# A hybrid attention, SSM and MoE block: masks behind the first rows, own tiles for the second half of x, two tiles for C, three for uT

## The chip, the cores and the metric

The kernel runs on one core of a Trainium2 chip. The metric is the device time of one execution in microseconds; the median of three executions of the kernel before is 1205.27 us (1204.71, 1205.27 and 1208.66). TensorE (PE) runs at one of two clock levels, 1.2 or 2.4 GHz; a view by stretches of time gives the clock that was granted, as a share of the higher one.

## The reference

One block over x of 1024 rows (S) by 1024 columns (D), all in float32:

```python
h = _rmsnorm(x, norm_mix_g[l])
z = h @ w_in[l]
q, k, v, f, u_ssm, g_attn, g_ssm = jnp.split(z, splits, axis=-1)
...
y_attn = _forgetting_attention(q, k, v, f + b_forget[l]).reshape(b, s, D_ATTN)
y_ssm = _s5(u_ssm, ...)
mixed = (jax.nn.sigmoid(g_attn) * (y_attn @ w_proj_attn[l])
         + jax.nn.sigmoid(g_ssm) * (y_ssm @ w_proj_ssm[l]))
x = x + mixed @ w_out[l]
x = x + _hier_moe(_rmsnorm(x, norm_ffn_g[l]), ...)
```

The forgetting attention has 8 heads of 64; its logits take the running sum over time of log sigmoid of f. The S5 part has 32 groups of 16 channels with 64 complex states each, driven by u and read out by the complex matrix C. The MoE has 32 experts of width 256, two for each row.

## The kernel before, in words

A product in full precision is made of three matmuls: each operand is split into a high part (rounded to fp32r) and a low part, and high by high, low by high and high by low are added up in PSUM. So x after its norm is kept transposed as `hTh[k]` and `hTl[k]` (k = 0 to 7, 128 columns of D each), and every weight as a pair such as `wuh` and `wul`.

The front (lines 104 to 260) loads x in eight row tiles of 128 x 1024 (`x_load`, four buffers). `normalize` does for each tile: sum of squares on ACT (line 203), the mean on DVE (204), the power on POOL (206, `rstd`), the multiplication on DVE (207). `turn_x` transposes the four row tiles of one half at one k on PE (line 212, through PSUM tiles `psB_t`), ACT writes `hTh` (213), DVE writes `hTl` (214). `split_u` splits the weights of u (lines 221 to 224). `products_u` makes u^T for one k and one half of the rows: four m by three matmuls (229 to 231, tiles `psA_t`) and two for the forget logits (232, 233). ACT and DVE are put in the written order within the first half (`manual_schedule`); everywhere else a scheduler orders each engine's instructions by its own priorities.

The second half of x uses the same four buffers, so its loads stand behind the first half's transposes. From line 263 on come the coefficients of the SSM on DVE and ACT (`exp_acc`, `wrap`, sines at 342), the two parts of C (lines 351 to 361: `cin`, one buffer, transposed on PE at 359), then the products of the second half, and `store_u`, which copies u from PSUM to `uS` (DVE 242, ACT 244) and the forget logits to `FL` and `Fa` (245, 246). Four stores write `uS` to `u_d` (451). The forget sums (459 to 483) work on 8 partitions: exponential, logarithm, a scan over time.

The SSM stage (486 to 613) has four blocks b of 8 groups. `load_u(b)` brings u back as `uT` in eight DMAs (498); `uT` has two buffers, so block b + 2 is loaded at the end of block b. DVE, POOL and ACT build for each block phases `v`, `w`, sines `SI` and cosines `CO` (516 to 524), and the matrices `HQ` and `PT` (535 to 537, with `tq` on POOL); PE transposes `PT` (575), ACT copies it to `Pm` (579), PE multiplies `uT` by it (582), DVE turns the result (562, 564), scans it (594) and turns it back (`zc`), and PE reads it out (602, 603). Sixteen runs of the gate products (`gate_run`, lines 182 to 184, 48 matmuls each, results `ge` copied by ACT at 186) stand between these on PE, with `wgh` and `wgl` split from `raw_g` (171, 172). Behind follow the GLU, the attention, the output projection and the MoE. SP issues most DMAs, in order.

Of the kernel before, what the change touches and what calls it, by code (L numbers as in the profile page):

```python
# [10 lines left out]
F32 = mybir.dt.float32  # L11
# [31 lines left out]
def hybrid_block(ctx: ExitStack, tc: tile.TileContext, t, out):  # L43
# [63 lines left out]
    def x_load(i):  # L107
        x_ = xp.tile([P, D], F32, name="x", bufs=4)
        nc.sync.dma_start(x_, t["x"][i * P:(i + 1) * P, :])
        return x_  # L110
# [9 lines left out]


# [3 lines left out]
    for o in range(2):  # L125
# [10 lines left out]

    tri = cp.tile([P, P], F32, name="tri")
    nc.gpsimd.memset(tri, 1.0)
    nc.gpsimd.affine_select(tri, tri, pattern=[[1, P]], compare_op=ALU.is_gt, fill=0.0,
                            base=0, channel_multiplier=-1)  # L140

    mask_s = cp.tile([P, 256], BF16, name="mask_s")
    nc.gpsimd.memset(mask_s, 0.0)
    nc.gpsimd.affine_select(mask_s, mask_s, pattern=[[1, 256]], compare_op=ALU.is_ge, fill=NEG,
                            base=-128, channel_multiplier=-1)

    mask_m = cp.tile([P, P], BF16, name="mask_m")
    nc.gpsimd.memset(mask_m, 0.0)
    nc.gpsimd.affine_select(mask_m, mask_m, pattern=[[-1, P]], compare_op=ALU.is_ge, fill=NEG,
                            base=0, channel_multiplier=1)  # L150
    bfor = cp.tile([H, 1], F32, name="bfor")
    nc.gpsimd.dma_start(bfor, t["b_forget"].rearrange("(p o) -> p o", o=1))

    gk2 = cp.tile([P, 1], F32, name="gk2")
    gqt = cp.tile([P, 1], F32, name="gqt")
    for o in (0, 64):
        nc.gpsimd.dma_start(gk2[o:o + 64], t["k_norm_g"].rearrange("(p o) -> p o", o=1))
        nc.gpsimd.dma_start(gqt[o:o + 64], t["q_norm_g"].rearrange("(p o) -> p o", o=1))
# [31 lines left out]
    uS = [xp.tile([P, 8, P], F32, name=f"uS{m}") for m in range(4)]  # L190
# [3 lines left out]
    nc.gpsimd.memset(f32(wf), 0.0)  # L194
    FL = fp.tile([H, S], F32, name="FL")
    Fa = fp.tile([H, S], F32, name="Fa")
# [51 lines left out]
    with tc.manual_schedule(engines={mybir.EngineType.Activation, mybir.EngineType.DVE}):  # L248
        normalize(xs)
        for k in range(KD):  # L250
            if k % 2 == 0:
                split_u(k)
            first_half = turn_x(xs, k, halves[0])
    xs = [x_load(i) for i in range(4, NT)]
# [97 lines left out]
    for nm, dst in (("ssm_C_re", Cre), ("ssm_C_im", Cim)):  # L352
        cin = tp.tile([P, 4, 2, 64], F32, name="cin")
        src = t[nm].rearrange("(b a) c p -> (a c) b p", a=8)
        nc.sync.dma_start(cin[:, :, 0, :], src)
        nc.sync.dma_start(cin[:, :, 1, :], src)
        ps = smtile()
        for b in range(4):
            nc.tensor.transpose(ps[:, b * P:(b + 1) * P],
                                cin[:, b].rearrange("q o p -> q (o p)"), ident)  # L360
        nc.scalar.copy(dst.rearrange("p g c -> p (g c)"), ps)
# [64 lines left out]
    for k in range(5, KD):  # L426
        products_u(k, pu, pf, halves[0])
        turn_x(xs, k, halves[1])
    store_u(pu, pf, 0)
# [56 lines left out]
    with ExitStack() as st:  # L486
# [8 lines left out]
        def load_u(b):  # L495
            uT = wp2.tile([P, GB, P], F32, name="uT", bufs=2)
            for tau in range(8):
                nc.sync.dma_start(uT[CG * tau:CG * tau + CG],
                                  u_d[b * P:(b + 1) * P, tau, :].rearrange("(g c) j -> c g j", c=CG))
            uTs.append(uT)  # L500

        load_u(0)
        load_u(1)
        for m in range(3):
            gate_run(m)
        for b in range(G // GB):
# [102 lines left out]
            if b < 2:  # L609
                load_u(b + 2)  # L610
# [905 lines left out]
```

## Time and profile before

| what | value |
|---|---|
| median of three executions | 1205.27 us |
| the profiled execution's own time | 1208.14 us |
| its span in the profile | 1206.4 us |
| PE busy | 1116.5 us (93%) |
| DVE busy | 793.5 us (66%) |
| ACT busy | 619.5 us (51%) |
| POOL busy | 432.1 us (36%) |
| read from and written to HBM | 164.30 and 35.52 MB |

The profile is one execution. Busy time of PE counts matmuls whose ends are modelled and overlap; a share of 93% over the span is a mean over stages. The waits of an engine are listed by what released it, and the timeline gives each instruction's start with the idle time before it in brackets.

### The profile page before, as it was taken

The page shows a single profiled execution, that of the slowest core. Times are in us where ns is not written, and L with a number is a line of the kernel's source. Part 1 is how long each engine was busy: PE and PEld are TensorE (multiplying, and loading weights), DVE is VectorE, ACT ScalarE, POOL GpSimd, SP SyncE. Part 2 cuts the span into 40 slices and gives each one's busy share as a digit, 9 for nine tenths or more (in the row PEclk, how much of TensorE's full clock was granted, in tenths as well). Part 3 has the DMA queues.
Part 4 walks back from the last instruction along what each step waited for, and adds up shares of the span by engine and source line. Part 5 has one row for each costly group of instructions (what it writes and reads, how often), then busy time and mean ns, then how long its engine had stood idle before and what let it go on. Part 6 is the DMA issues. An engine that isn't in the chain of part 4 may idle for free. (4 is left out here: it accounts for less than half of the span.)

```text
span 1206.4 us, 15940 instructions
## 1 busy us (share of the span) xinstructions
PE 1116.5 (93%) x5323; PEld 854.3 (71%) x5324; DVE 793.5 (66%) x1561; ACT 619.5 (51%) x1195; POOL 432.1 (36%) x431
## 2 busy tenths in 40 slices
PE   5899899899999999999899988998499999999995
PEld 4678778687898778888677777886366666666562
DVE  4657577667025889898987696538566666666661
ACT  5423332332335576766769553103366666666662
POOL 3025445432514474656714362103322222222211
PEclk9899899999999999999989999999699999999998
DMA  8516435330253012000622539564599999999992
GB/s 234 82 41 157 92 75 104 80 91 28 87 121 53 2 27 47 11 23 28 210 70 101 175 124 346 189 220 179 185 306 341 333 312 317 312 310 320 310 332 51
DMA packets 100919, 193.78 MB, mean 161 GB/s; under 512 B 26177, under 2 KB 55169, under 8 KB 100833
## 3 DMA queue, kind: packets, MB, share of 16 engines
q1 hardware_dynamic: 82176, 150.16, 40.8%
q0 software_dynamic: 14048, 34.17, 10.5%
q10 hardware_dynamic: 4608, 8.39, 1.9%
q8 instruction: 43, 0.70, 0.2%
q14 instruction: 44, 0.35, 0.1%
HBM read 164.30 MB, written 35.52 MB: 166 GB/s over the span
## 5 line engine op out<-in xcount | busy, mean ns | idle before, releaser
L1102 DVE TENSOR_TENSOR wel<-raw_e,weh 128x512 fp32r<-128x512 f32 x256 | 157.4, 684 | 118.8 <-ACT weh L1101 107.5
L1101 ACT CAST weh<-raw_e 128x512 fp32r<-128x512 f32 x256 | 137.0, 621 | 3.0 <-DMA raw_e<-in_w_expert_up 1.8
L910 POOL TENSOR_TENSOR sm<-sm,pe 128x256 f32<-128x256 f32 (+2 forms) x80 | 96.4, 1205 | 72.5 <-ACT pe L907 64.2
L1377 PE MATMUL psA_t<-wd,hT 128*96 128x512 f32 x256 | 117.4, 600 | 3.1 <-DMA wd<-in_w_expert_down 2.3
L1352 PE MATMUL psA_t<-weh,xh 128*96 128x512 f32 x256 | 103.7, 405 | 0.2
L1353 PE MATMUL psA_t<-wel,xh 128*96 128x512 f32 x256 | 102.0, 399 | 0.0
L183 PE MATMUL psA_t<-hTh,wgl 128*128 128x512 f32 x256 | 101.9, 398 | 0.0
L182 PE MATMUL psA_t<-hTh,wgh 128*128 128x512 f32 x256 | 101.4, 396 | 0.0
L1354 PE MATMUL psA_t<-weh,xl 128*96 128x512 f32 x256 | 101.2, 395 | 0.0
L184 PE MATMUL psA_t<-hTl,wgh 128*128 128x512 f32 x256 | 100.8, 394 | 0.0
L1379 POOL DMA_INDIRECT out_rows<-R,ix x32 | 46.1, 1441 | 128.5 <-ACT hT L1368 117.2
L793 PE MATMUL psA_t<-wqh,hTh 128*128 128x384 f32 x256 | 88.3, 345 | 0.0
L794 PE MATMUL psA_t<-wql,hTh 128*128 128x384 f32 x256 | 86.8, 339 | 0.0
L795 PE MATMUL psA_t<-wqh,hTl 128*128 128x384 f32 x256 | 86.8, 339 | 0.0
L1328 POOL DMA_INDIRECT XG<-xn_d,ix x32 | 36.5, 1140 | 139.7 <-PE psB_t L1339 132.3
L1378 ACT ACTIVATE R<-psA_t,wts 96x512 f32<-96x512 f32 x64 | 43.7, 682 | 77.1 <-PE psA_t L1377 75.0
L1377 PEld LDWEIGHTS psA_t<-wd,hT 128*96 128x96 f32 x256 | 40.4, 168 | 56.4 <-issue 49.0
L905 ACT ACTIVATE pH<-psB_t 128x512 fp32r<-128x512 f32 (+1 forms) x96 | 49.1, 512 | 38.9 <-PE psB_t L902 38.7
L908 DVE TENSOR_TENSOR pL<-pe,pH 128x256 fp32r<-128x256 f32 (+2 forms) x80 | 62.9, 798 | 6.8 <-ACT pe L907 5.9
L855 DVE TENSOR_REDUCE mx<-psB_t 128x1 f32<-128x512 f32 (+2 forms) x96 | 51.2, 550 | 7.9 <-PE psB_t L850 4.2
L183 PEld LDWEIGHTS psA_t<-hTh,wgl 128*128 128x128 f32 x256 | 48.7, 190 | 9.5 <-POOL wgl L172 0.2
L184 PEld LDWEIGHTS psA_t<-hTl,wgh 128*128 128x128 f32 x256 | 48.5, 189 | 9.5
(427 smaller groups left out, 2878.2 us busy)
## 6 DMA issues: line engine op xcount, KB each, us to landing
raw_e<-in_w_expert_gate SPq DMA_DIRECT2D x64, 512.0 KB
raw_e<-in_w_expert_up SPq DMA_DIRECT2D x64, 512.0 KB
wd<-in_w_expert_down SPq DMA_DIRECT2D x64, 512.0 KB
gate_d<-ge ACTq DMA_DIRECT2D x32, 256.0 KB
gt<-gate_d SPq DMA_DIRECT2D x16, 512.0 KB
raw_g<-in_w_in SPq DMA_DIRECT2D x12, 512.0 KB
raw_q<-in_w_in SPq DMA_DIRECT2D x48, 128.0 KB
x<-in_x SPq DMA_DIRECT2D x8, 512.0 KB
```

What stands on the lines that cost most here:

```text
L182: nc.tensor.matmul(ps, wh, hTh[k][:, ns], start=(k == 0), stop=False)
L183: nc.tensor.matmul(ps, wl, hTh[k][:, ns], start=False, stop=False)
L184: nc.tensor.matmul(ps, wh, hTl[k][:, ns], start=False, stop=(k == KD - 1))
L793: nc.tensor.matmul(ps[:, :384], ah, wh, start=(k == 0), stop=False)
L794: nc.tensor.matmul(ps[:, :384], ah, wl, start=False, stop=False)
L910: nc.gpsimd.tensor_tensor(sm[:, o0:], sm[:, o0:], pe[:, :n], ALU.add)
L1101: nc.scalar.copy(wh[d_], src)
L1102: nc.vector.tensor_tensor(wl[d_], src, f32(wh[d_]), ALU.subtract)
L1352: nc.tensor.matmul(ps, xh[:, k, :], wh[:, k % 2, :], start=(k == 0), stop=False)
L1353: nc.tensor.matmul(ps, xh[:, k, :], wl[:, k % 2, :], start=False, stop=False)
L1354: last = nc.tensor.matmul(ps, xl[:, k, :], wh[:, k % 2, :], start=False, stop=(k == KD - 1))
L1377: pe = nc.tensor.matmul(po, hT[:, j, :], wd[j][:, ns], start=(j == 0), stop=(j == 1))
```

## The change

It does five things. (1) The four row tiles of the second half of x get their own buffers, in a ring (`tag="uS"`) that the four `uS` tiles take over once the last transposes have read them; their loads are issued straight behind those of `raw_u`. (2) The POOL work for `tri`, `mask_s`, `mask_m` and the five small POOL DMAs (`bfor`, `gk2`, `gqt`) is written behind the first half, and the zeroing of `wf` behind the first half's `normalize`. (3) `FL` and `Fa` become rows 0 to 7 and 32 to 39 of one tile. (4) `cin` gets two buffers. (5) `uT` gets three buffers: blocks 0 to 2 are loaded ahead of block 0, block 3 at the end of block 0.

```diff
     def x_load(i):
-        x_ = xp.tile([P, D], F32, name="x", bufs=4)
+        x_ = xp.tile([P, D], F32, name="x" if i < 4 else "x2", tag="x" if i < 4 else "uS", bufs=4)
         nc.sync.dma_start(x_, t["x"][i * P:(i + 1) * P, :])
...
+    xs2 = [x_load(i) for i in range(4, NT)]
...
-    tri = cp.tile([P, P], F32, name="tri")
...
-    uS = [xp.tile([P, 8, P], F32, name=f"uS{m}") for m in range(4)]
+    uS = []
...
-    nc.gpsimd.memset(f32(wf), 0.0)
-    FL = fp.tile([H, S], F32, name="FL")
-    Fa = fp.tile([H, S], F32, name="Fa")
+    FL = fp.tile([64, S], F32, name="FL")
+    FL, Fa = FL[0:H], FL[32:32 + H]
...
         normalize(xs)
+        nc.gpsimd.memset(f32(wf), 0.0)
...
-    xs = [x_load(i) for i in range(4, NT)]
+
+    tri = cp.tile([P, P], F32, name="tri")
...
+    xs = xs2
...
-        cin = tp.tile([P, 4, 2, 64], F32, name="cin")
+        cin = tp.tile([P, 4, 2, 64], F32, name="cin", bufs=2)
...
+    uS.extend(xp.tile([P, 8, P], F32, name="uS", tag="uS", bufs=4) for m in range(4))
     store_u(pu, pf, 0)
...
-            uT = wp2.tile([P, GB, P], F32, name="uT", bufs=2)
+            uT = wp2.tile([P, GB, P], F32, name="uT", bufs=3)
...
-        load_u(0)
-        load_u(1)
+        for b in range(3):
+            load_u(b)
...
-            if b < 2:
-                load_u(b + 2)
+            if b < 1:
+                load_u(b + 3)
```

The scheduler then orders the first stages anew. ACT in the first half, before (`hTh_151` to `hTh_154` are k = 4 to 7; `x` with line 203 is the second half):

```order
L213 ACTIVATE hTh_151<-psB_t,gmix 128x512
L213 ACTIVATE hTh_152<-psB_t,gmix 128x512
L221 CAST wuh<-raw_u 128x1024
L222 CAST wf<-raw_u 128x2x8
L213 ACTIVATE hTh_153<-psB_t,gmix 128x512
L203 ACTIVATE junk,ss<-x 128x1024
L213 ACTIVATE hTh_154<-psB_t,gmix 128x512
L203 ACTIVATE junk,ss<-x 128x1024 x3
```

In these rows the second half's squares follow k = 6 and 7. The same place of ACT after the change (`hTh_136` to `hTh_139` are k = 2 to 5; `x_109` to `x_115` are the second half's tiles):

```order
L190 ACTIVATE hTh_136<-psB_t,gmix 128x512
L180 ACTIVATE junk,ss<-x_109 128x1024
L190 ACTIVATE hTh_137<-psB_t,gmix 128x512
L180 ACTIVATE junk,ss<-x_111 128x1024
L198 CAST wuh<-raw_u 128x1024
L199 CAST wf<-raw_u 128x2x8
L190 ACTIVATE hTh_138<-psB_t,gmix 128x512
L180 ACTIVATE junk,ss<-x_113 128x1024
L190 ACTIVATE hTh_139<-psB_t,gmix 128x512
L180 ACTIVATE junk,ss<-x_115 128x1024
```

The squares of the second half now stand between k = 2 and 5 of the first, each ahead of a later `hTh`. PE at the transposes of the second part of C, before (`hTh_152` is k = 5, `hTh_153` k = 6):

```order
L232 MATMUL psB_t<-hTh_152,wf 128x512
L233 MATMUL psB_t<-hTl_160,wf 128x512
L229 MATMUL psA_t<-hTh_153,wuh 128x512
L230 MATMUL psA_t<-hTh_153,wul 128x512
L359 MATMUL psB_t<-ident,cin 128x128 x4
L212 MATMUL psB_t<-ident,x 128x128 x4
L231 MATMUL psA_t<-hTl_161,wuh 128x512
```

Four transposes of `cin` stand inside k = 6. PE at both parts of C after the change (`hTh_138` is k = 4, `hTh_139` k = 5):

```order
L209 MATMUL psB_t<-hTh_138,wf 128x512
L210 MATMUL psB_t<-hTl_146,wf 128x512
L189 MATMUL psB_t<-ident,x_109 128x128
L189 MATMUL psB_t<-ident,x_111 128x128
L189 MATMUL psB_t<-ident,x_113 128x128
L189 MATMUL psB_t<-ident,x_115 128x128
L360 MATMUL psB_t<-ident,cin 128x128 x8
L206 MATMUL psA_t<-hTh_139,wuh 128x512
```

All eight transposes of `cin` now stand together ahead of k = 5. DVE behind the products of u, before:

```order
L172 TENSOR_TENSOR wgl<-raw_u,wgh 128x1024 x2
L242 COPY uS_164<-psA_t 128x64x8
L242 COPY uS_166<-psA_t 128x64x8
L246 SCALAR_TENSOR_TENSOR FL<-psB_t,bfor,Fa 8x512
L461 SCALAR_TENSOR_TENSOR Fa<-FL 8x1024
L464 SCALAR_TENSOR_TENSOR FL<-FL,Fa 8x1024
L516 TENSOR_TENSOR v<-phh,j_628 128x1024
L473 SCALAR_TENSOR_TENSOR Fa<-Fm,FL 8x1024
L282 TENSOR_SCALAR w<-v 128x1024
```

The forget sums (461, 464, 473) follow the last `uS` copies and are mixed with the phase `v`. DVE at the same place after the change:

```order
L150 TENSOR_TENSOR wgl<-raw_u,wgh 128x1024
L463 SCALAR_TENSOR_TENSOR FL<-FL 8x1024
L466 SCALAR_TENSOR_TENSOR FL<-FL 8x1024
L150 TENSOR_TENSOR wgl<-raw_u,wgh 128x1024
L475 SCALAR_TENSOR_TENSOR FL<-Fm,FL 8x1024
L476 SCALAR_TENSOR_TENSOR FL<-Fo,FL 8x32
L478 TENSOR_TENSOR FL<-FL 8x992
L481 SCALAR_TENSOR_TENSOR Fm<-FL,Fh 8x1024
L219 COPY uS<-psA_t 128x64x8 x2
L518 TENSOR_TENSOR v<-phh,j_623 128x1024
```

The whole of the forget sums (463 to 481) moved ahead of the last two `uS` copies, and `v` follows these.

## Rows read from the trace of the kernel before

**Rows 1.** From the page, the busy time of PE: us, share of the span, instructions.

```profile
PE 1116.5 (93%) x5323; PEld 854.3 (71%) x5324; DVE 793.5 (66%) x1561; ACT 619.5 (51%) x1195; POOL 432.1 (36%) x431
```

**Rows 2.** The waits of PE from 0 to 300 us: what waited, what it waited for, then us in total, how many times, and the longest.

```profile
PE psB_t L212 <- DVE ss L204: 10.2, 3, 9.5
PE psB_t L582 <- ACT Pm L579: 8.6, 3, 4.0
PE psB_t L359 <- DMA cin<-in_ssm_C_im: 4.8, 1, 4.8
PE psB_t L603 <- POOL zc L565: 3.0, 4, 1.0
PE psB_t L212 <- DVE dt_n L271: 2.4, 1, 2.4
PE psA_t L229 <- DVE uS L242: 1.3, 1, 1.3
```

**Rows 3.** Busy time by stretches: the stretch and its length, then the busy time of PE, PEld, DVE, ACT and POOL (instructions), the granted clock of PE, the share of the DMA engines, GB/s.

```profile
88.20:124.10 35.90, 35.90 (x169) 29.24 (x167) 29.09 (x24) 13.67 (x16) 19.12 (x9) 1.00 0.71 172
128.00:134.10 6.10, 6.08 (x25) 5.69 (x25) 2.76 (x4) 0.58 (x1) 5.94 (x9) 0.50 0.30 51
...
175.50:181.50 6.00, 5.95 (x36) 5.17 (x37) 5.40 (x8) 0.59 (x1) 5.55 (x10) 1.00 0.96 132
...
870.00:1200.00 330.00, 319.75 (x1318) 198.19 (x1316) 192.28 (x338) 217.78 (x434) 74.07 (x60) 0.99 0.93 297
```

**Rows 4.** PE in the timeline: start, length, line, instruction, and in brackets the idle time before it and what ended it.

```profile
26.66 0.39 PE L231 MATMUL psA_t<-hTl,wuh 128*128 128x512 f32 x1
26.88 0.39 PE L229 MATMUL psA_t<-hTh,wuh 128*128 128x512 f32 x1
...
31.06 0.41 PE L212 MATMUL psB_t<-ident,x 128*128 128x128 f32 x2 [2.43 <-DVE dt_n L271]
...
35.16 0.39 PE L231 MATMUL psA_t<-hTl,wuh 128*128 128x512 f32 x1
...
50.64 1.09 PE L359 MATMUL psB_t<-ident,cin 128*128 128x128 f32 x4 [4.85 <-DMA cin<-in_ssm_C_im]
...
55.70 0.39 PE L230 MATMUL psA_t<-hTh,wul 128*128 128x512 f32 x1
...
69.72 0.50 PE L229 MATMUL psA_t<-hTh,wuh 128*128 128x512 f32 x1 [1.32 <-DVE uS L242]
...
128.02 2.08 PE L582 MATMUL psB_t<-uT,Pm 128*128 128x128 f32 x8 [3.80 <-ACT Pm L579]
...
134.02 0.50 PE L184 MATMUL psA_t<-hTl,wgh 128*128 128x512 f32 x1
...
148.56 0.49 PE L603 MATMUL psB_t<-HQ,zc 128*128 128x128 f32 x2 [1.04 <-POOL zc L565]
...
152.01 0.49 PE L603 MATMUL psB_t<-HQ,zc 128*128 128x128 f32 x2 [0.47 <-POOL zc L565]
...
175.55 1.16 PE L582 MATMUL psB_t<-uT,Pm 128*128 128x128 f32 x8 [0.84 <-ACT Pm L579]
...
178.79 0.48 PE L183 MATMUL psA_t<-hTh,wgl 128*128 128x512 f32 x1
```

**Rows 5.** POOL in the timeline, from 7 us.

```profile
7.13 0.99 POOL L194 MEMSET wf<- 128x1024 f32 x1
8.04 0.62 POOL L206 TENSOR_TENSOR rstd<-ss,mhalf 128x1 f32<-128x1 f32 x1
```

**Rows 6.** The loads of the second half of x, first SP's in the timeline (from the issue of the first to that of the last), then ACT at the first of their squares.

```profile
21.89 2.60 SPq L109 DMA_DIRECT2D x<-in_x  x4
...
26.85 1.06 ACT L203 ACTIVATE junk<-x 128x1024 f32<-128x1024 f32 x1 [5.02 <-DMA x<-in_x]
```

**Rows 7.** The timeline of SP, DVE and ACT from 42 to 58 us, at the load of the second part of C, the wait of DVE behind it, and the first copy to `uS`.

```profile
42.18 0.37 SPq L355 DMA_DIRECT2D cin<-in_ssm_C_im  x1
...
53.34 0.75 DVE L214 SCALAR_TENSOR_TENSOR hTl<-psB_t,gmix,hTh 128x512 fp32r<-128x512 f32 x1 [5.17 <-ACT hTh L213]
...
57.95 1.08 ACT L244 COPY uS<-psA_t 128x512 f32<-128x512 f32 x1
```

**Rows 8.** The timeline of DVE and then of ACT, from the end of the products of u to the first `Pm`.

```profile
89.64 1.52 DVE L461 SCALAR_TENSOR_TENSOR Fa<-FL 8x1024 f32<-8x1024 f32 x1
...
97.14 1.21 DVE L516 TENSOR_TENSOR v<-phh,j 128x1024 f32<-128x1024 f32 x1
...
114.69 2.65 DVE L520 TENSOR_SCALAR CO<-v 128x1024 f32<-128x1024 f32 x1
...
121.43 0.69 DVE L282 TENSOR_SCALAR w<-CO 128x1024 f32<-128x1024 f32 x1
...
121.43 1.15 ACT L522 ACTIVATE SI<-v,sgn 128x1024 f32<-128x1024 f32 x1 [8.31 <-DVE v L283]
...
127.40 0.57 ACT L579 COPY Pm<-psB_t 128x512 f32<-128x512 f32 x1
```

**Rows 9.** SP and ACT in the timeline: the loads of `uT` for blocks 0 and 1, the next loads of gate weights, and the first cast that reads those.

```profile
92.47 18.02 SPq L498 DMA_DIRECT2D uT<-u_d  x16
114.80 0.39 SPq L103 DMA_DIRECT2D raw_g<-in_w_in  x1
...
140.50 1.05 ACT L171 CAST wgh<-raw_g 128x1024 fp32r<-128x1024 f32 x1 [1.91 <-DMA gate_d<-ge]
```

More of the change, by code (lines that the diff above doesn't have):

```diff
@@ L135, in hybrid_block @@
     nc.vector.memset(mhalf, -0.5)
-    tri = cp.tile([P, P], F32, name="tri")
[L138 to L158, printed above, removed]
     negF_d = tc.dram_tile([H, 4, S], F32, name="negF_d")
@@ L253, in hybrid_block @@
             first_half = turn_x(xs, k, halves[0])
-    xs = [x_load(i) for i in range(4, NT)]
+    tri = cp.tile([P, P], F32, name="tri")
+    nc.gpsimd.memset(tri, 1.0)
+    nc.gpsimd.affine_select(tri, tri, pattern=[[1, P]], compare_op=ALU.is_gt, fill=0.0,
+                            base=0, channel_multiplier=-1)
+    mask_s = cp.tile([P, 256], BF16, name="mask_s")
+    nc.gpsimd.memset(mask_s, 0.0)
+    nc.gpsimd.affine_select(mask_s, mask_s, pattern=[[1, 256]], compare_op=ALU.is_ge, fill=NEG,
+                            base=-128, channel_multiplier=-1)
+    mask_m = cp.tile([P, P], BF16, name="mask_m")
+    nc.gpsimd.memset(mask_m, 0.0)
+    nc.gpsimd.affine_select(mask_m, mask_m, pattern=[[-1, P]], compare_op=ALU.is_ge, fill=NEG,
+                            base=0, channel_multiplier=1)
+    bfor = cp.tile([H, 1], F32, name="bfor")
+    nc.gpsimd.dma_start(bfor, t["b_forget"].rearrange("(p o) -> p o", o=1))
+    gk2 = cp.tile([P, 1], F32, name="gk2")
+    gqt = cp.tile([P, 1], F32, name="gqt")
+    for o in (0, 64):
+        nc.gpsimd.dma_start(gk2[o:o + 64], t["k_norm_g"].rearrange("(p o) -> p o", o=1))
+        nc.gpsimd.dma_start(gqt[o:o + 64], t["q_norm_g"].rearrange("(p o) -> p o", o=1))
+    xs = xs2
     pu, pf = [mmtile() for _ in range(4)], smtile()
```

## The prediction

> **What bounds the kernel now.** I read the page first: PE is busy 93% of the span [rows 1], so the time is PE's work plus its waits, and a change that adds no PE work can only give back waits or slow stretches. Next the waits of PE in the first 300 us [rows 2]; the reader should see that the front and the first SSM blocks hold nearly all that this change can touch: the first transposes wait 9.5 us for the norm, one transpose 2.4 for the second half of x, one 4.8 for the second part of C, three matmuls 8.6 for `Pm`, four 3.0 for `zc`. Then the stretches [rows 3]: PE is busy for all of 88.2 to 124.1 at a granted clock of 1.00, but behind a wait of 3.80 the clock was 0.50, the lower of the two levels, from 128.0 to 134.1. Last the timeline of PE [rows 4], for the price of a wait: it is the idle time and the slow stretch behind it. At full clock a product of 128x512 starts every 0.2275 us or so (26.66 to 26.88 shows one step), a transpose of 128x128 takes some 0.09 (the eight matmuls of line 582 at 175.55, 128x128 too, take 0.99 until the next).
>
> All times below are of the profiled execution, 1208.14 us by its own time, 2.87 above the median of the three, 1205.27. I forecast a difference and subtract it from the median.
>
> **A. POOL at the start.** The first `rstd` starts at 8.04, held by the masks, five DMAs and the zeroing of `wf` [rows 5]. In the new order the zeroing still stands ahead of the first `rstd`, and the masks and DMAs now stand between the four. All four squares follow the landing of x, so only the last chain counts, and between the `rstd`s POOL has room for one mask or two DMAs each. The last one comes perhaps 0.5 us earlier: -0.5. Bounds: -1.0 (the `wf` zeroing 0.99 no longer in the way) and +1.5: a TENSOR_SCALAR of 128x1024 took 2.65 us at 114.69 beside work of POOL, one at 121.43 took 0.69 [rows 8], and should the last row tile's multiplication stretch like that beside a mask, it ends 2 us later. The Trainium skill has the reason for this and speaks against this part of the change (GPSIMD Engine Reference, Specifications): POOL shares its interfaces to SBUF with VectorE, and they contend in some modes of DVE. The trace agrees with it in these two rows; by the rule the sum would be 2 us worse, by the value that I take it is not, since behind the last `rstd` no mask is left in POOL's new order.
>
> **B. The second half of x.** Before, its loads are issued at 21.89, and the first square waits 5.02 us, to 26.85 [rows 6]. After, they stand right behind `raw_u` and wait for no transposes, so they should land well before 26.85; I reckon with 8 us, most of the distance from issue to last square. The transposes that waited 2.43, to 31.06, then have their data nearly in time. From 31.06 to 35.16 stand 6 products and 6 transposes: 6 x 0.2275 + 6 x 0.09 = 1.9 us of work in 4.10, so 2.2 more are given back by the clock. DVE is in order, and its multiplications follow the first half's last `hTl`, which the old trace has at about the time when PE's wait began (31.06 - 2.43 = 28.6), so small waits stay, which I put at 0.45: -2.43 - 2.2 + 0.45 = -4.2. Bounds: -4.6 (no wait stays) and -2.2 (a wait of that length stays and the clock falls all the same).
>
> **C. The second part of C.** With one `cin` its load waits for the transposes of the first part, is issued at 42.18 [rows 7], and PE waits 4.85 for it, to 50.64. With two it is issued together with the first part's, ahead of the gate weights, and the transposes stand together. From 50.64 to 55.70 stand 8 transposes and 8 products: 0.7 + 1.8 = 2.5 us in 5.06. So -4.85 - 2.5 = -7.35. Nothing replaces it: the load then has some 20 us. Bounds: -7.4 and -4.85.
>
> **D. The turn from the first half of the products to the second.** Before, PE goes from one to the other with a wait of 1.32 (69.72) for a copy of `uS`, without loss of clock. After, the second half's products start with eight of the forget logits, some 1.8 us, and then need a bank that ACT frees by its first `uS` copy; ahead of that in ACT's order stands the second sine, which needs DVE's coefficients. These were held 5.17 us by the in-order wait of DVE at 53.34 [rows 7], a wait that goes with C, but the products come earlier by about as much as C and B give. By the distances of the old rows ACT is free at about 52.9 and PE there at 50.6: a wait of 2.3 for the 1.32. It is close to the wait of 2.43 that cost 2.2 by the clock; the one of 1.32 cost none; I take 1.75. So -1.32 + 2.3 + 1.75 = +2.7. Bounds: -1.3 and +4.
>
> A to D make -0.5 - 4.2 - 7.35 + 2.7 = -9.35 by the end of the products of u.
>
> **E. SSM block 0.** Its chain on DVE starts with `v` at 97.14, behind forget sums from 89.64 on [rows 8]: 7.5 us, and the scan and others are mixed in behind. They now stand ahead of the last `uS` copies, in a stretch where DVE waits for PE. ACT's `SI` waits 8.31 for that chain, and `ge`, `Ka` and `Pm` are queued behind it; `Pm` at 127.40 ends PE's wait of 3.80. With 7.5 us less ahead of it the chain needs 3.5 to remove the wait but for 0.3. The work from 128.02 to 134.02 (two rounds of line 582, one of 575, four products) takes 178.79 - 175.55 = 3.24 in block 1, at clock 1.00: 2.76 more. So -3.5 - 2.8 = -6.3. Bounds: -6.6, and 0 if `HQ`, whose tiles wait for the stores of u, holds the chain in place of the forget sums.
>
> **F. `zc`.** The waits 1.04 and 0.47 at 148.56 and 152.01 [rows 4] follow DVE's scans, and in the old order a `wgl` stands ahead of the first scan; now it stands behind the second. -1.5; bounds -1.5 and 0.
>
> **G. Block 1.** Its chain to `Pm` starts with the same DVE work and does not get shorter, so where PE no longer waits for `zc`, it comes to `Pm` that much too early: the 0.84 at 175.55 becomes about 2.1. +1.3; bounds 0 and, with a slow stretch as in E, +4.
>
> Parts 3 and 5 of the change as such I price at nothing: the `FL` operations keep their lengths, and the third `uT` moves a load that no row of PE waits for. Behind block 1 the new order is the old one but for a few swaps, and the late stage (DMA share 0.93, PE 320 of 330 us [rows 3]) starts earlier by as much, its loads following the buffers that it frees itself.
>
> **Sum:** -9.35 - 6.3 - 1.5 + 1.3 = -15.85, so 1192.3 for the profiled execution and 1205.27 - 15.85 = **1189.4** for the median.
>
> **Rivals.** R1, the front alone: the stores of u and `HQ`, not the forget sums, set block 0's chain, or ACT and POOL do; E and F give nothing and G asks nothing, and A to D lose a little: -8, 1197.3. For it: the chain holds much besides the forget sums (SI's wait of 8.31 ends 24 us behind `v`); against: 7.5 us stand straight ahead of `v`. R2, more: D costs nothing and its 1.32 goes too (4.0 better), and block 2, whose wait of 4.0 [rows 2] is untouched above, gives half of it because its `uT` is loaded early: 1189.4 - 6 = 1183.4. R3, given back later: `Pm` in blocks 1 and 2 takes all of it, since the coefficient chains on DVE, not PE, set the SSM stage: DVE is busy 29 of 35.9 us where PE waits for nothing [rows 3]. Then the time stays within a few us, 1204. R4, slower: 24 loads of `uT` now stand in SP's queue ahead of the gate weights. Sixteen took 18.0 us to issue, 1.13 each, and a load issued behind them at 114.80 was cast at 140.50 [rows 9]: 25.7 us of slack, of which E and F take 7.8. At 2.8 us an issue the 24 take 67, and the gate weights are issued 4 + 67 = 71 us behind the products of u in place of 26.6: 45 later, less 18 of slack is 27 that PE waits, and with the 15.85 gained elsewhere +11, 1216. It decides from 2.3 us an issue. Against: nothing in the change makes an issue longer than 1.13, and at that the 24 end no later than 16 did.
>
> **Chances.** Forecast 0.58 (its own range 1185 to 1194, by the bounds of D, E and G), R1 0.20, R2 0.10, R3 0.07, R4 0.05. A measurement here tells a change from none at about 0.3%, 3.6 us. Faster: forecast, R1 and R2, 0.88; same: R3, 0.07; slower: R4, 0.05. A range of 1182 to 1200 holds the forecast, R1 and R2 but for their edges, and leaves out R3, R4 and some of those.
>
> **What would show it.** In the new trace: no wait of PE for `cin` (C); the transposes of the second half's x with waits under 0.6 (B); a new wait at the first `uS` bank of about 2.3 (D); the first gate product near 79 (before, the stretch without a wait begins at 88.2); the first `Pm` wait under 1 with the clock at 1.00 behind it (E); `zc` waits gone and the second `Pm` wait near 2 (F, G). It would be wrong if the first `Pm` wait stays near 3.8, or if ACT's squares between k = 2 and 5 hold `hTh` so that PE waits within the first half's products.

## The result, and the profile after

The changed kernel takes 1195.19 us (median of seven, 1191.27 to 1198.39) against 1205.27 of the kernel before (seven, 1199.9 to 1208.66): a ratio of 0.9912, 95% interval 0.989 to 0.9934. It is faster by some 10 us; the forecast was 1189.4, 16 us faster, with a range of 1182 to 1200. The profiled execution took 1195.19 by its own time, with a span of 1193.5.

On the page, the busy time of PE, which answers to [rows 1]:

```profile
PE 1111.4 (93%) x5323; PEld 851.5 (71%) x5324; DVE 795.3 (67%) x1561; ACT 620.3 (52%) x1195; POOL 431.3 (36%) x431
```

The waits of PE from 0 to 300 us in the changed kernel, which answer to [rows 2] (line 189 is 212 of before, 584 is 582, 604 and 605 are 602 and 603, 206 and 208 are 229 and 231):

```profile
PE psB_t L189 <- DVE ss L181: 9.9, 3, 7.5
PE psB_t L584 <- ACT Pm L581: 6.0, 2, 4.5
PE psB_t L189 <- DVE hTl L191: 2.3, 1, 2.3
PE psB_t L604 <- DMA Mt<-Ka: 2.3, 1, 2.3
PE psB_t L605 <- POOL zc L567: 1.5, 2, 1.0
PE psA_t L208 <- DVE hTl L191: 1.0, 1, 1.0
PE psA_t L206 <- ACT uS L221: 0.9, 1, 0.9
```

The wait for the second part of C (4.8) is gone, and so is one of the three waits for `Pm`. Two are new, 2.3 and 1.0 for `hTl`, and the one for `Mt` has grown from 0.8 to 2.3. Where they stand shows in the timeline of PE:

```profile
15.38 1.22 PE L206 MATMUL psA_t<-hTh,wuh 128*128 128x512 f32 x2
...
24.67 0.66 PE L189 MATMUL psB_t<-ident,x 128*128 128x128 f32 x4 [2.33 <-DVE hTl L191]
...
28.82 0.39 PE L208 MATMUL psA_t<-hTl,wuh 128*128 128x512 f32 x1
...
56.66 0.50 PE L206 MATMUL psA_t<-hTh,wuh 128*128 128x512 f32 x1 [0.93 <-ACT uS L221]
...
64.79 0.50 PE L208 MATMUL psA_t<-hTl,wuh 128*128 128x512 f32 x1 [1.03 <-DVE hTl L191]
...
118.02 1.07 PE L584 MATMUL psB_t<-uT,Pm 128*128 128x128 f32 x8
...
138.38 0.49 PE L605 MATMUL psB_t<-HQ,zc 128*128 128x128 f32 x2
...
161.88 1.16 PE L584 MATMUL psB_t<-uT,Pm 128*128 128x128 f32 x8 [1.48 <-ACT Pm L581]
...
179.01 0.77 PE L604 MATMUL psB_t<-Mt,uT 128*128 128x128 f32 x2 [2.30 <-DMA Mt<-Ka]
...
182.47 0.38 PE L605 MATMUL psB_t<-HQ,zc 128*128 128x128 f32 x2
...
210.95 1.44 PE L584 MATMUL psB_t<-uT,Pm 128*128 128x128 f32 x5 [4.52 <-ACT Pm L581]
```

Against [rows 4]: the first product starts at 15.38, not earlier than before. The wait of 2.43 for the second half of x is gone, and a wait of 2.33 at 24.67, inside the first half of the products, is there instead, with slow products until 28.82. The first `Pm` matmul, at 118.02, has no bracket: no wait. Block 1 waits 1.48 for `Pm` (0.84 before) and 2.30 for `Mt`, and behind the latter the products are slow until 182.47. In the kernel before, the wait for `Mt` was 0.77:

```profile
191.40 0.46 PE L602 MATMUL psB_t<-Mt,uT 128*128 128x128 f32 x2 [0.77 <-DMA Mt<-Ka]
```

The stretches, columns as in [rows 3]:

```profile
118.00:124.10 6.10, 6.10 (x38) 5.26 (x38) 4.80 (x8) 0.59 (x1) 5.93 (x10) 1.00 0.86 141
161.80:167.80 6.00, 5.92 (x36) 5.16 (x37) 5.81 (x8) 0.61 (x2) 5.55 (x10) 1.00 0.94 85
178.00:184.00 6.00, 4.99 (x25) 4.49 (x25) 0.00 (x0) 0.00 (x0) 1.11 (x1) 0.72 0.01 3
```

Behind the first `Pm` the clock is now 1.00 (0.50 before). From 178 to 184 it is 0.72.

With the starts of four matmuls the way of PE falls into stages: the first product of u, the first gate product, the second group of `zc` matmuls in block 0, and the first transpose of the output stage of the SSM. Each number is a difference of starts in the timeline (before: 15.20, 88.06, 152.01, 283.09; after: 15.38, 81.70, 138.38, 273.61):

| stage | before | after | forecast change | change |
|---|---|---|---|---|
| to the first product (A) | 15.20 | 15.38 | -0.5 | +0.2 |
| products of u (B, C, D) | 72.86 | 66.32 | -8.85 | -6.5 |
| gate runs and block 0 (E, F) | 63.95 | 56.68 | -7.8 | -7.3 |
| block 0's end to the output stage (G) | 131.08 | 135.23 | +1.3 | +4.2 |
| sum to the output stage | 283.09 | 273.61 | -15.85 | -9.5 |
| from there to the span's end | 923.3 | 919.9 | 0 | -3.4 |

The last line is scatter: over all 14 profiles of this study it lies between 917.8 and 925.3, without any order by what was edited, and two profiles of the same kernel differ there by 2.9 and by 4.1.

A second profile of the changed kernel, in the runs below, has the stages 15.40, 64.71, 56.67, 133.79 and 922.7, so it starts the output stage at 270.57, 12.5 earlier than before the change and not 9.5. The difference to the first profile stands at the two waits of above:

```profile
23.73 0.66 PE L189 MATMUL psB_t<-ident,x 128*128 128x128 f32 x4 [1.07 <-DVE hTl L191]
...
177.38 0.46 PE L604 MATMUL psB_t<-Mt,uT 128*128 128x128 f32 x2 [2.28 <-DMA Mt<-Ka]
```

```profile
176.40:182.40 6.00, 5.02 (x33) 4.57 (x34) 0.00 (x0) 1.01 (x2) 1.10 (x1) 1.00 0.01 3
```

The wait in the first half of the products is 1.07 in place of 2.33, the one for `Mt` is as long as in the first profile, and behind neither was the clock below 1.00. A landmark of a single profile can thus be off by 1.6 us in the front and by 3.0 at the output stage.

### The profile page after: what moved, and what is told of

Read it like the earlier page. It is cut to its first block, busy times and chain, and to the rows that moved or that the text cites. A ratio compares the mean times of both kernels' runs of the same rounds, so it can differ in the third digit from the quotient of the medians.

```text
span 1193.5 us, 15934 instructions
## 1 busy us (share of the span) xinstructions
PE 1111.4 (93%) x5323; PEld 851.5 (71%) x5324; DVE 795.3 (67%) x1561; ACT 620.3 (52%) x1195; POOL 431.3 (36%) x431
## 5 line engine op out<-in xcount | busy, mean ns | idle before, releaser
L796 PE MATMUL psA_t<-wql,hTh 128*128 128x384 f32 x256 | 86.3, 337 | 0.0
L160 PEld LDWEIGHTS psA_t<-hTh,wgh 128*128 128x128 f32 x256 | 48.5, 190 | 10.0 <-DVE uS L219 0.5
L1163 PE MATMUL psA_t<-woh,mxh 128*128 128x512 f32 x128 | 54.3, 424 | 1.2 <-DVE gt L988 1.2
```

The source lines that it names most:

```text
L160: nc.tensor.matmul(ps, wh, hTh[k][:, ns], start=(k == 0), stop=False)
L796: nc.tensor.matmul(ps[:, :384], ah, wl, start=False, stop=False)
```

## The experiments

**The squares on ACT.** Theory 1 for the loss among the products: the scheduler put the squares of the second half on ACT between k = 2 and 5 of the first, and their data lands too late. The timeline of ACT in the changed kernel:

```profile
16.83 0.70 ACT L190 ACTIVATE hTh<-psB_t,gmix 128x512 fp32r<-128x512 f32 x1
22.11 1.06 ACT L180 ACTIVATE junk<-x 128x1024 f32<-128x1024 f32 x1 [4.58 <-DMA x<-in_x]
...
23.16 0.67 ACT L190 ACTIVATE hTh<-psB_t,gmix 128x512 fp32r<-128x512 f32 x1
```

The first square waits 4.58 us for its load; behind it in order stands `hTh` of k = 3, which thus starts at 23.16 in place of some 17.5. DVE's `hTl` follows it, a PSUM tile comes free late, and PE waits 2.33. The other squares wait for no load: ACT had no idle time ahead of them. The prediction had reckoned with the first some 3 us earlier (26.85 less 8). The experiment holds the squares behind `hTh` of k = 3:

```diff
-        nc.scalar.activation(hTh[k][:, hs], ps, AF.Copy, scale=gmix[:, k:k + 1])
+        last_h.append(nc.scalar.activation(hTh[k][:, hs], ps, AF.Copy, scale=gmix[:, k:k + 1]))
...
-    with tc.issue_after(first_half.ins):
+    with tc.issue_after(first_half.ins), tc.issue_after(last_h[3].ins):
         normalize(xs)
```

> The changed kernel, with the squares of the second half of x held on ACT behind the first half's hTh of k = 3 (in the changed kernel the first of them stands ahead of it). Theory 1: in the changed kernel the first square waits for its load until 22.1 us and holds hTh of k = 3, so that PE waits 2.33 us at 24.7 and is slow behind it; then here this wait is under 0.7, the slow products behind it are mostly gone, and the first gate product starts 3.5 to 4.5 us earlier than 81.7, at 77.2 to 78.2. Rival: the early 2 MB of x hold back the weights of u, and no order on ACT helps; then the first gate product stays at 81 to 82.5. The forget sums stay early on DVE, so what comes behind should move by as much: a span 3 to 4 us below that of the changed kernel by theory 1, within 1 by the rival.

1193.65 us (1187.38 to 1196.34), 0.9877 of before (0.984 to 0.9914). Its waits of PE from 0 to 300 us:

```profile
PE psB_t L586 <- ACT Pm L583: 6.3, 3, 4.5
PE psB_t L191 <- DVE x L184: 2.6, 3, 1.5
PE psB_t L606 <- DMA Mt<-Ka: 2.3, 1, 2.3
```

No wait for `hTl` at a transpose is left in the first half (nearly all of the 2.6 for `x` stands ahead of the first product); the first gate product starts at 78.99, 2.7 earlier than in the changed kernel's first profile, less than expected, and 1.1 earlier than in its second. The products of u take 63.64, for 66.32 and 64.71. Theory 1 holds for the wait, which is gone; its size differs between two profiles of the changed kernel by as much as the experiment gains on the second. At the output stage (270.38) the gain shows against the first profile alone, and the span is 1.9 lower, which the scatter of the late stage covers.

Then all four squares behind k = 7 (`last_h[-1]` in place of `last_h[3]`):

> As the run before, but with all four squares behind the last hTh of the first half (k = 7). Here the scheduler also puts the forget sums on DVE and ACT behind the last copies of u again, as in the kernel before the change. Theory 1 of the squares and theory E of the forget sums together: no wait in the first half of the products, first gate product at 76 to 78, and then the wait for the first Pm comes back, 3 to 4 us, with a clock of 0.5 behind it, so that the first zc matmul is 20 us behind the first Pm and not 16.5; the time then about that of the changed kernel (within 3 us). Rival: the forget sums aren't what the first Pm waited for; then its wait stays under 1 us and the time is 4 us below the changed kernel.

1197.91 us (1195.31 to 1203.29), 0.9914 (0.9888 to 0.994). The products of u take 61.12 and the first gate product starts at 76.44, 5.3 earlier than in the changed kernel. Then the forget sums, late again in this order, take it back: the wait for the first `Pm` is 4.58, and the stage to the second `zc` group takes 63.98, as before the change. Both theories together, as expected, but for a wait somewhat above the 3 to 4 us.

**The own tiles for x alone,** on the kernel before (the hunks for `x_load`, `xs2` and `uS`, nothing else). Here the scheduler puts the first square behind k = 0:

> The kernel before the change, with the own tiles and early loads of the second half's x alone. In this order the first of its squares stands on ACT already behind hTh of k = 0 and the others ahead of k = 2 to 4; the forget sums stand early, as in the changed kernel. Theory 1 (squares in order on ACT): hTh of k = 1 waits for the load that lands at about 22, PE waits 3 to 6 us for it between 18 and 26 with a slow stretch behind; the waits for the second half (2.43) are gone, the one for cin (about 4.8) is not; the first gate product at 87 to 91, so no gain in the front. Theory E: no wait for the first Pm. Together the time is 2 to 7 us below before. Rival: the early loads help as such, since ACT gets to the squares late enough; then no wait over 1.5 us in the first half and the first gate product at 83 to 85.

1200.62 us (1198.88 to 1202.96), 0.9951 (0.9928 to 0.9974). The waits of PE in the timeline, and the first square on ACT:

```profile
24.06 1.12 PE L214 MATMUL psB_t<-ident,x 128*128 128x128 f32 x4 [3.88 <-DVE hTl L216]
...
51.45 0.88 PE L361 MATMUL psB_t<-ident,cin 128*128 128x128 f32 x3 [2.87 <-DVE t L284]
```

```profile
21.50 1.06 ACT L205 ACTIVATE junk<-x 128x1024 f32<-128x1024 f32 x1 [6.34 <-DMA x<-in_x]
```

PE waits 3.88 in the first half, and the first gate product starts at 89.33, later than before the change. The wait for C shrinks from 4.85 to 2.87, and it is now put down to `t` on DVE, which gets to it late. The gain, 5.5 us, lies behind: 57.11 to the second `zc` group where the kernel before has 63.95, since this part alone is what moves the forget sums ahead.

**The second buffer for C alone,** on the kernel before, with the packed tile for `FL` and `Fa`. The packing frees the 4 KB of a partition that the second `cin` and the third `uT` need; without it SBUF holds neither.

```diff
-    FL = fp.tile([H, S], F32, name="FL")
-    Fa = fp.tile([H, S], F32, name="Fa")
+    FL = fp.tile([64, S], F32, name="FL")
+    FL, Fa = FL[0:H], FL[32:32 + H]
...
-        cin = tp.tile([P, 4, 2, 64], F32, name="cin")
+        cin = tp.tile([P, 4, 2, 64], F32, name="cin", bufs=2)
```

> The kernel before the change, with the second buffer for cin and the packed FL tile that makes room for it; nothing else. Theory C: the wait of 4.85 us for the second part of C and the slow stretch of 2.5 behind it go and nothing replaces them: the first gate product at 80 to 81.5 (88.06 before), the waits of 2.43 and 1.32 and that of the first Pm (3.8) stay. Time 6 to 8 us below before. Rival: the coefficients' chain or the turn to the second half takes the place of the wait; then a new wait of over 1 us appears between 50 and 75 us, and the first gate product comes at 82.5 or later.

1200.07 us (1196.98 to 1202.04), 0.9944 (0.9928 to 0.9961). The wait of 4.85 is gone, the others stay (2.33, 1.40, 4.57 for the first `Pm`), and the first gate product starts at 82.04, 6.0 earlier. That is 1.3 short of the term C. The stretches show where it went:

```profile
30.70:36.00 5.30, 5.30 (x16) 3.78 (x17) 3.67 (x17) 1.15 (x2) 1.72 (x3) 0.54 0.92 101
36.00:50.00 14.00, 14.00 (x71) 11.68 (x71) 12.02 (x69) 7.09 (x10) 0.00 (x0) 0.93 0.82 123
```

Behind the wait for x, of 2.33 here and 2.43 before, the clock was low until 35.2 before; here it still is beyond 36 (0.93 over 36 to 50; the last product that started 0.43 behind the one ahead of it did so at 37.72). The same wait has not the same price in two kernels.

**The forget sums.** The changed kernel, with the forget sums' DVE work queued behind the last copy of `uS`:

```diff
-                nc.vector.tensor_copy(dst, src)
+                last_u.append(nc.vector.tensor_copy(dst, src))
...
-        forget_sums()
+        with tc.issue_after(last_u[-1].ins):
+            forget_sums()
```

> The changed kernel, with the forget sums' DVE work held behind the last copy of u on DVE; nothing else is edited. Theory E: the early forget sums are what removed PE's wait for the first Pm (3.80 before the change, none after) and the slow stretch behind it; then the first gate product stays at 81 to 82.5, the wait for the first Pm is 3 to 4.5 us, and the way from the first gate product to the first zc matmul grows from 52.8 to 58 to 60.5 (60.5 before the change). Rival 1: the stores of u or ACT and POOL set this chain; then the wait stays under 1 us and the time stays within 1 us of the changed kernel's spans.

1200.57 us (1198.11 to 1204.88), 0.9936 (0.9912 to 0.996). The waits of PE from 0 to 300 us, and the first `Pm` matmul in the timeline:

```profile
PE psB_t L587 <- ACT Pm L584: 10.4, 4, 4.5
...
PE psB_t L607 <- DMA Mt<-Ka: 2.1, 1, 2.1
```

```profile
120.15 1.22 PE L587 MATMUL psB_t<-uT,Pm 128*128 128x128 f32 x4 [4.09 <-ACT Pm L584]
```

The waits for `Pm` make 10.4 us where the changed kernel has 6.0; the first, at 120.15, is 4.09, and the way from the first gate product to the second `zc` group is 63.05 in place of 56.68. By the expectation's measure, the first `zc` matmul, it is 59.17 in place of 52.79. So the order that this one edit leads to is worth 6.4 us in this stage; the two times alone, with intervals that overlap, would not show it. Theory E held and rival 1 fell, though the first gate product came at 79.89 and not at 81 to 82.5: PE's wait in the front was 1.23 here, without an edit there. Yet rival 1 had a point. DVE in the changed kernel:

```profile
85.09 1.21 DVE L481 SCALAR_TENSOR_TENSOR Fm<-FL,Fh 8x1024 f32<-8x1024 f32 x1 [1.13 <-ACT Fh L480]
...
88.21 2.40 DVE L518 TENSOR_TENSOR v<-phh,j 128x1024 f32<-128x1024 f32 x1
93.80 1.36 DVE L537 TENSOR_TENSOR HQ<-U1g,Cre 128x1152 f32<-128x1152 f32 x1 [3.19 <-ACT ge L164]
```

The forget sums end at 86.3, 4.6 behind the first gate product, and the last `uS` copies wait for them; so `v` comes at 88.21, 6.5 behind that product. Before it was 9.1 (97.14 [rows 8] less 88.06): 2.6 nearer, not 7.5. Then `HQ` waits 3.19, which this profile puts down to `ge` on ACT (done long before). SP issues the last three stores of u between 87.30 and 91.09, and the other seven profiles with early forget sums name these stores for the same wait; the changed kernel's second one:

```profile
91.69 1.36 DVE L537 TENSOR_TENSOR HQ<-U1g,Cre 128x1152 f32<-128x1152 f32 x1 [2.70 <-DMA u_d<-uS]
```

Scan, sums and `Fm` no longer stand between `v` and `CO`, so `CO` comes 22.8 behind the first gate product in place of 26.6. A further 2.2 come from `w`, the instruction behind `CO`. Before the change, with POOL's `wgl` from 116.75 to 119.58 beside it, and after:

```profile
117.26 2.88 DVE L282 TENSOR_SCALAR w<-v 128x1024 f32<-128x1024 f32 x1
```

```profile
106.93 0.68 DVE L283 TENSOR_SCALAR w<-v 128x1024 f32<-128x1024 f32 x1
```

In the changed kernel POOL's `wgl` starts at 112.49, when `w` has long ended. All six profiles with late forget sums have 2.88 here and `wgl` beside it, all eight with early ones 0.68. So ACT's `SI` comes 6.2 nearer to the first gate product, 2.2 of it by an order on POOL that goes with the forget sums and that no experiment held apart from them.

**The third uT.** The prediction priced it at nothing. The changed kernel with two:

```diff
-            uT = wp2.tile([P, GB, P], F32, name="uT", bufs=3)
+            uT = wp2.tile([P, GB, P], F32, name="uT", bufs=2)
...
-        for b in range(3):
-            load_u(b)
+        load_u(0)
+        load_u(1)
...
-            if b < 1:
-                load_u(b + 3)
+            if b < 2:
+                load_u(b + 2)
```

> The changed kernel with two buffers for uT in place of three and the loads of blocks 2 and 3 back at the end of blocks 0 and 1. Theory U: the third uT (its eight more loads in SP's queue, and the order of PE that goes with it) is why block 1 waits more than before the change, 1.48 us for Pm and 2.30 for Mt with a slow stretch behind; then here both waits are back at about 0.8 without a slow stretch, the first gate product stays at 80 to 82.5, and the start of the output stage (273.61 in the changed kernel) comes 2 to 3.5 us earlier. Rival: PE only arrives earlier at chains that don't get shorter; then the waits stay at 1.5 and 2.3 and the output stage comes as far behind the first gate product as in the changed kernel, 191.9, within 0.7.

1191.74 us (1188.95 to 1194.49), 0.9873 (0.9846 to 0.99). Its first gate product is at 80.49, its output stage starts at 270.66, 2.95 earlier than in the changed kernel's first profile and no earlier than in its second (270.57); the way from block 0's end is 132.72, for 135.23 and 133.79. Block 1 waits 0.85 and 0.92, where both profiles of the changed kernel have 1.48 and 2.3. And the kernel before with three, one execution (1209.93 us, beside 1206.78 as the median of before):

> The kernel before the change, with the third uT and the packed FL tile that makes room for it. Theory U: the third uT costs in block 1 here too; the way from the first gate product to the output stage, 195.0 before, is 196.5 to 197.5, with the waits of 1.5 for Pm and above 2 for Mt in block 1 in place of 0.84 and 0.77. Rival: it costs only together with the other parts; then 194.5 to 195.5.

Its waits of PE, where [rows 2] has 8.6 for `Pm`:

```profile
PE psB_t L582 <- ACT Pm L579: 10.6, 3, 4.6
...
PE psB_t L602 <- POOL zc L565: 2.4, 1, 2.4
```

The way from the first gate product to the output stage is 199.0, more than either theory expected: it costs 4 here. Over all 14 profiles, from the second `zc` group of block 0 to the output stage the seven with three `uT` take 133.8 to 136.0, the seven with two 131.1 to 132.7, whatever else they have. The means are 135.1 and 131.9.

That is not all cost, for the third `uT` also gives something in block 0. The kernel with two, from its list of waits:

```profile
PE psB_t L605 <- POOL zc L567: 3.0, 4, 1.0
```

These are four waits for `zc`, where the changed kernel has two. The two in block 0 (1.05 and 0.48) are back: all seven profiles with two `uT` have them and a `wgl` ahead of the first scan on DVE, all seven with three have neither. So the swap of `wgl` that term F counted on goes with the third `uT`, not with the forget sums. From the first gate product to the output stage the means are 191.4 with three and 189.7 with two beside early forget sums, 199.2 and 195.0 beside late ones: a net cost of 1.8 and of 4.1.

Where it arises: with early forget sums, counted from the first gate product, PE gets `Mt` in block 1 at 97.3 with three and at 96.6 to 97.2 with two, nearly the same. But without the `zc` waits PE is there 0.7 to 1.1 earlier, so it waits 2.3 in place of 0.9 to 1.1, in one piece, and behind that longer wait six of the seven profiles with three have slow products. This is nearer to the rival's mechanism (PE arrives earlier at a chain that doesn't get shorter) than to theory U's, although theory U's numbers came. The profile of the kernel with the third `uT` alone names `zc` on POOL for the wait, but the waiting instruction does not depend on `zc`; it depends on the eight loads of `Mt`. Loads and order were not held apart by an experiment.

**The masks.** On the kernel before, alone, one execution (1208.15 us):

> The kernel before the change, with the masks, the small DMAs of POOL and the zeroing of wf moved as in the change, and nothing else. Theory A, as corrected by the changed kernel's trace (first product at 15.38 with the DMAs between the rstds): no gain, the first product at 15.2 to 15.6 and the first gate product at 87.5 to 89.5. Rival: the part is worth 0.5 to 1.5 us by itself, with the first product at 14.7 or earlier.

First product at 15.42, as theory A corrected has it; the first gate product at 86.47, 1.6 earlier than before and 1.0 outside the range of theory A. Its wait for x (2.43) is gone, and the one for C is longer:

```profile
53.02 1.09 PE L359 MATMUL psB_t<-ident,cin 128*128 128x128 f32 x4 [7.27 <-DMA cin<-in_ssm_C_im]
```

7.27 in place of 4.85: the load of C is issued at 42.09 (42.18 before [rows 7]), and what PE gained ahead of it, it waits there. Why the start gained nothing is to be seen on POOL in the changed kernel:

```profile
10.71 0.58 POOL L183 TENSOR_TENSOR rstd<-ss,mhalf 128x1 f32<-128x1 f32 x1
11.23 0.95 POOL L253 DMA_DIRECT2D gk<-in_k_norm_g  x1
12.18 0.52 POOL L254 DMA_DIRECT2D gqt<-in_q_norm_g  x1
12.71 0.57 POOL L183 TENSOR_TENSOR rstd<-ss,mhalf 128x1 f32<-128x1 f32 x1
```

Between the third and the fourth `rstd` stand two small DMAs, 1.47 us, and the fourth starts at 12.71, though the first starts at 5.92 in place of 8.04 [rows 5]. The fourth before the change:

```profile
12.55 0.55 POOL L206 TENSOR_TENSOR rstd<-ss,mhalf 128x1 f32<-128x1 f32 x1 [0.93 <-DVE ss L204]
```

With the masks and DMAs held behind the fourth `rstd`:

```diff
+    with tc.issue_after(last_r[3].ins):
+        tri = cp.tile([P, P], F32, name="tri")
...
```

> The changed kernel with the masks and the five small DMAs of POOL held behind the fourth rstd. In the changed kernel the DMAs stand between the rstds and the fourth multiplication starts at 13.31, the first product at 15.38. Both theories: the fourth rstd follows its mean directly, and the first product starts at 13.2 to 14.2. Theory 1: the end of the first half hangs on the landing of the second half's x at 22, ahead of hTh of k = 3 on ACT, so PE gives the gain back there: its wait of 2.33 grows by as much, and the first gate product stays at 81 to 82. Rival: the wait stays as long as it is and the first gate product comes 1.2 to 2.2 us earlier, at 79.5 to 80.5.

1195.81 us (1190.11 to 1196.94), 0.9904 (0.9871 to 0.9936). The first product starts at 14.35, 1.0 earlier and less than both theories said; the first gate product at 78.35, 3.35 earlier than in the first profile of the changed kernel and more than either (1.8 earlier than in the second). Neither was right: the landing of x moved too, and no wait is left at the transposes of the first half, though the squares stand where they stood. The first square on ACT here:

```profile
19.44 1.06 ACT L182 ACTIVATE junk<-x 128x1024 f32<-128x1024 f32 x1 [2.93 <-DMA x<-in_x]
```

**Three edits together:** squares behind k = 3, POOL work behind the fourth `rstd`, two `uT`.

> The changed kernel with three edits together: the squares behind hTh of k = 3, the POOL masks and DMAs behind the fourth rstd, and two uT as before. If the theories hold: first product at 13.2 to 14.2, no wait over 1 us in the first half, first gate product at 76.5 to 78 (81.70 in the changed kernel), block 1 with waits of 0.8, the start of the output stage at 266 to 268.5 (273.61), the span 5 to 7.5 us below the changed kernel's. If the gains swallow each other: first gate product at 78.5 or later, output stage at 270 or later.

1189.45 us (1183.56 to 1192.14), 0.9854 (0.9818 to 0.9891). First product at 13.82, first gate product at 76.86, output stage at 266.06. The landmarks came as expected. None of the three edits alone is clear of the changed kernel in time, since their intervals overlap with its own, and alone each starts the output stage at 270.3 to 270.7, where the changed kernel's second profile does (270.57; the first 273.61); together it is 266.06. That single gains add up is thus not shown one by one, only that the three together gain. It was run again, beside the changed kernel on the same chip:

> The changed kernel itself, once more, to stand beside the run with three edits on the same chip, and to see how far its landmarks move from one profile to the next. All theories: ratio to before 0.989 to 0.9935; first square of the second half of x at 21 to 22.5 us, the wait behind it 1.2 to 2.4, the first gate product at 80 to 82.5, 191.4 to 192.4 from there to the output stage.

> The kernel with three edits (squares behind hTh of k = 3, POOL work behind the fourth rstd, two uT) once more, with more rounds. Expected 1187 to 1191, a ratio to before of 0.983 to 0.988, and 4 to 8 us below the changed kernel beside it; if the better landmarks up to 270 us are lost later on, less than 3 us below it.

The changed kernel: 1195.71 us (1193.05 to 1198.41, six), 0.9896 (0.9868 to 0.9924). Three edits: 1190.26 (1187.80 to 1192.72, six), 0.9844 (0.9818 to 0.987). The slowest with three edits is faster than the fastest of the changed kernel; the medians differ by 5.5 us, and the output stage starts at 266.13, for 270.57. The waits of PE with three edits:

```profile
PE psB_t L589 <- ACT Pm L586: 5.1, 2, 4.3
PE psB_t L610 <- POOL zc L572: 3.0, 4, 1.1
...
PE psB_t L609 <- DMA Mt<-Ka: 1.1, 1, 1.1
```

The changed kernel's second profile missed two expectations: a wait of 1.07 behind the first square, where 1.2 to 2.4 was expected, and 190.46 from the first gate product to the output stage, where 191.4 to 192.4 was expected, since there was no slow stretch behind `Mt`.

## Why the prediction was right, and where not

The direction and the range were right, and so was most of the way; the size was 1.6 times what came, and the forecast's own range, 1185 to 1194, was missed by 1.2. To the output stage the two profiles of the changed kernel gain 9.5 and 12.5 of the 15.85.

A (-0.5) came out as +0.2. The step that failed is "between the `rstd`s POOL has room for one mask or two DMAs each": two DMAs took 1.47 us and held the last `rstd`. Held behind it, they give 1.0 at the first product. The bound of +1.5, a multiplication slowed beside a mask, was far too wide: the first took 0.93 beside the masks, the fourth 0.75 in both kernels, and 0.91 where the masks run beside the fourth.

B (-4.2) is where most of the front's shortfall is. The wait of 2.43 went as foreseen. But the prediction reckoned with a landing of x 8 us earlier than 26.85, and took the squares between `hTh`s for harmless; they held `hTh` of k = 3 for a landing at 22.1, and PE paid 2.33 and slow products from 24.67 to 28.82. In the second profile the landing was at 21.17 and PE paid 1.07 alone. With C at -7.35 and D as below, B by difference is +0.2 in the first profile and -1.5 in the second. The prediction's end named this as what would make it wrong. With the squares one or more steps later the products of u take 63.64 or 61.12, for the 64.0 (72.86 less 8.85) that B, C and D forecast together. The 0.09 of a transpose in B and C is not what the row named for it gives (0.99 for eight matmuls is 0.12), but it holds: the four transposes of line 575 that follow there take 0.36, from 176.54 to 176.90.

C (-7.35) measured -6.0 alone: the wait went whole, the slow stretch behind the wait ahead of it grew. In the changed kernel the clock is 1.00 from 28.9 to 118, so wait and slow stretch both went.

D (+2.7) was too dear. The turn has two waits, 0.93 and 1.03, for the 1.32, and no slow stretch: +0.6.

E and F (-7.8) measured -7.3, and -6.4 by the experiment on E alone. The six orders with late forget sums take 63.0 to 64.0 for this stage, the eight profiles with early ones 56.7 to 57.5. But the working was partly luck: `v` came only 2.6 us nearer, not 7.5, and took 2.40 in place of 1.21; R1's stores do hold `HQ`; and 2.2 of what the chain gained came from `w`, no longer beside POOL's `wgl`, which the prediction did not look at. F's waits went, by the swap of `wgl` that it named, but that order came with the third `uT`, priced at nothing; and without them the stage is only 0.4 to 0.8 shorter.

G (+1.3) with the third `uT` at nothing is the other step that failed: +4.2 and, in the second profile, +2.7. The runs with two `uT` and early forget sums take 131.7 to 132.7 for the 131.1 of before, without the cause that G names, since their `zc` waits are there; with three they take 133.8 to 135.3, some 2.5 more by the means. G had the mechanism, PE early at block 1's chain, and found it at `Pm` (1.48 for a forecast 2.1); the larger part came at `Mt` (2.30 for 0.77), which the prediction did not look at, and in the slow products behind it. "It moves a load that no row of PE waits for" was true of the load, and not of the orders that changed with it.

The rivals: R1 (1197.3) lies nearer to the measured 1195.19 than the forecast, but E and F gave what R1 denied them, and the time came out there for other reasons. R2's gain in block 2 did not come (4.52 for 4.0). R4's queue of 24 `uT` loads was no danger: they took 27.47 us to issue, 1.14 each, but a smaller cost of the same part was real.

## What to carry to other kernels

A load moved ahead is worth what the in-order engine does with it: look where the scheduler puts the first reader, and what waits behind that, before counting the old wait as a gain. Price each part of a change by the order it leads to, not by its own instructions: here own tiles for x paid mostly by moving 8-partition sums out of another chain, and a buffer that looked free gave a little in one block and cost more in the next, some 2 us net. Cut the way of the bound engine at the same few instructions in every profile; stages then repeat to within two us where the late stage, which nothing edited, scatters by over seven. And take a second profile of the kernel that you explain: here one wait went from 2.33 to 1.07, and the slow products behind two waits went, without an edit.

## What the runs showed of the hardware

Where POOL issued its five small DMAs (at most 0.2 KB each) ahead of the fourth `rstd`, the first square of the second half found its data at 21.2 to 22.1 (the six profiles, of five kernels, in which that square waited for its load, the kernel with x's own tiles alone among them); where it issued them behind (three profiles), at 19.0 to 19.4, though SP issued the loads of x in the same order. From 16 to 18 us the DMA engines were busy 0.72 and moved 261 GB/s in the changed kernel, 1.02 and 382 with the small DMAs behind. In the kernel with x's own tiles alone, where they come at 4.4 to 7.2, the dip is at 10 to 12 (0.70, 218 GB/s). A dip some 5 us behind the small DMAs fits these two; in the third the loads are nearly done by then. That the small DMAs cause it was not tested.

A TENSOR_SCALAR of 128x1024 on DVE (`w`) took 2.88 in the six profiles where POOL's `wgl` ran beside it and 0.68 in the eight where POOL did nothing at that time; beside POOL's masks one took 0.91 to 0.93 for 0.75.

PE's clock fell behind waits of 2.33, 2.30, 3.80 and 4.52 and not behind those of 0.93, 1.03, 1.32 and 1.48. The length of a wait does not settle it: behind a wait of 2.09 for `Mt` (forget sums late) the clock was 0.50, behind one of 2.28 at the same place (the changed kernel's second profile) it stayed at 1.00. How long it stayed low differed too: to 35.2 and to 37.7 behind nearly the same wait for x in two kernels.
